# Scan products of an SSD mixer on four 64 by 64 tiles of TensorE, the second token block stored with its halves swapped, and the sample's products apart on 32 columns

## The chip, the cores and the metric

The kernel runs on one core of one Trainium2 chip. Its time is the device time of one execution in microseconds (us); a version's time is the median of several executions on the same chip. Beside it stands a profile: one execution, recorded instruction by instruction, of which the quoted lines are a part. Engines go by their names in it: PE is TensorE (PEld its weight loads), DVE VectorE, ACT ScalarE, POOL GpSimd, SP SyncE.

## The reference

One layer of a streaming encoder for 256 tokens of a new stream (the prompt) and the next 32 tokens of a running one (the sample), with shared weights. The input is normed and multiplied by w_in; the columns of the result go to a pooling mixer, to a gate z, and to an SSD mixer of 32 heads of 64 channels in two groups. Both mixers' outputs go through w_out and then a ConvFFN. What the change touches is the scan of the SSD mixer, which the reference works out in chunks of 64 tokens with a state carried from chunk to chunk:

```python
cb = jnp.einsum('bclgn,bcsgn->bcgls', Cc, Bc)
y_diag = jnp.einsum('bcgls,bcgjls,bcsgjp->bclgjp', cb, lmat, xc)
...
h_last, h_prev = lax.scan(step, h0, ...)
y_off = jnp.einsum('bclgn,bcgjpn,bcgjl->bclgjp', Cc, h_prev, jnp.exp(acum))
y = (y_diag + y_off).reshape(b, s, G, J, P) + D[..., None] * xh
```

Written out without chunks, a head's output at token l is the sum over all tokens s up to l of (C_l . B_s) exp(-decay between s and l) dt_s x_s, plus the old state's part and D x_l. For the prompt the old state is zero; the sample has one.

## The kernel before

**Layout.** Activations stand with channels on the 128 partitions and the 288 tokens (256 and 32) along the row. `project` (L171) multiplies a chunk of 256 weight columns with all tokens into two accumulators of the PSUM pool `acc_ps` (five buffers): each weight block arrives as f32 by DMA (`raw`), ScalarE rounds it to a high part `whi` (L151), VectorE subtracts for the low part `wlo` (L152), and TensorE runs three passes for each (L165). Of `whi` and `wlo` there are four buffers each. The splits get high priority, so the scheduler places them ahead of other work.

**The scan.** A group q is four heads, eight groups in all. For each: `ssd_tokens` (L617) loads x transposed to tokens on partitions into `xk` (three blocks: tokens 0 to 127, 128 to 255, and the last 128, of which the last 32 count; L619 and L620 on GpSimd's queue; three buffers). `ssd_first` (L598) broadcasts the decay sums over partitions (`gb`, L601), loads the old state `h0t` and forms `ce` (L610). `ssd_masks` (L623) multiplies x by dt (L636), forms the exponentials on ScalarE (L643, L646) and multiplies them by the masked products of B and C, `cbt` (L648). The mask `m` of a head has 416 columns: 256 for the first block of tokens against all later outputs, 128 for the second against its own, 32 for the sample.

**The products.** `run_pair` (L796) runs four times, each time for two groups: after the x chunk 7 and after the z chunks 1, 4 and 6. `ssd_products` runs for each group two pairs of heads, the two heads of a pair on the two halves of TensorE's columns: 256 columns (L668), 128 columns for the second block (L670), then the sample's 32 columns from new tokens (L672) and from the old state (L674). These are f32 products, and their place in TensorE's order is pinned to the written one. `ssd_add` (L684) then adds D x and the product into `xs` on VectorE, once for the prompt and once for the sample. After that come the gate (L758 takes z from its accumulator, L764 and L767 multiply) and the norm.

What the scheduler may move (VectorE, ScalarE, GpSimd) it orders itself; TensorE's order is that of the text. Of other work around the scan, L434, L435, L449, L454 and L455 are the causal convolution of x, and L211 its transpose on the way to the token layout.

Of the kernel before, what the change touches and what calls it, by code (L numbers as in the profile page):

```python
# [8 lines left out]
F32 = mybir.dt.float32  # L9
F32R = mybir.dt.float32r  # L10
AF = mybir.ActivationFunctionType
ALU = mybir.AluOpType
# [3 lines left out]
P = 128  # L16
TC = {"schedule_with_timeline_sim": True}
D_MODEL = 2048
NP_ = 256
NS = 32  # L20
NT = NP_ + NS
# [3 lines left out]
HEADS = 32  # L25
# [4 lines left out]
NF = D_FF // P  # L30
NXC = CONV // P
NU = D_POOL // P
BLK = ((0, P), (P, P), (NP_, NS))
WINDOWS = (2, 4, 8, 16)
HALF = NF // 2
# [33 lines left out]
def body(  # L69
# [23 lines left out]
    act, dve, pool, pe, sp = nc.scalar, nc.vector, nc.gpsimd, nc.tensor, nc.sync  # L93
# [9 lines left out]
    acc_ps = ctx.enter_context(tc.tile_pool(name="acc_ps", bufs=5, space=PSUM))  # L103
# [3 lines left out]
    def aux(shape, name):  # L107
        return aux_ps.tile(shape, F32, tag="aux", name=name)
# [21 lines left out]
    pin = tc.keep_in_program_order  # L130
# [90 lines left out]
    start = ExitStack()  # L221
# [41 lines left out]
    for name, n in COLS:  # L263
# [12 lines left out]
    tri = const.tile([P, P], F32, name="tri")  # L276
    pool.affine_select(
        out=tri, in_=ones, pattern=[[1, P]], compare_op=ALU.is_ge, fill=0.0, base=0, channel_multiplier=-1
# [79 lines left out]
    for i, (kb, n) in enumerate(CHUNKS):  # L358
# [26 lines left out]
        for q, (r, m, k, x) in enumerate(products):  # L385
            if i == len(CHUNKS) - 1 and q == 0:
                p_ = aux([P, NT], "prs")
# [9 lines left out]
                start=kb + k + r + x == 0, stop=kb + k == KD - 1 and r == 1,  # L397
            ))

    for k in range(KD):  # L400
        c = slice(HEADS * (k % 4), HEADS * (k % 4 + 1))
# [90 lines left out]
    with tc.high_priority(offset=EVAC):  # L492
        for i, v in enumerate(v4):
            c = slice(HEADS * i, HEADS * (i + 1))
# [34 lines left out]
    r = htile("r", tag="z")  # L529
# [26 lines left out]
    tok = mp.tile([P, 3, 2, HEADS], F32, name="tok")  # L556
    tokd = const.tile([P, 3, HEADS], F32, name="tokd")
    p_t = aux([P, 9 * HEADS], "ptok")
    p_tok = p_t.rearrange("p (b h) -> p b h", b=3)
# [4 lines left out]
    act.activation(elast, g[:, 415:416], AF.Exp)  # L564
    e_d = dram.tile([HEADS, 1], F32, name="e_d")
    sp.dma_start(out=e_d, in_=elast)
    dve.tensor_copy(tok, p_tok[:, :, : 2 * HEADS].rearrange("p b (r h) -> p b r h", r=2))
    dve.tensor_copy(tokd, p_tok[:, :, 2 * HEADS :])
    wq = side2.tile([P, HEADS], F32, name="wq")
    for j in range(3):  # L570
# [4 lines left out]
    for i in range(4):  # L575
        o = btile("bc")
# [3 lines left out]
    cbt = mp.tile([P, 2, MW], F32, name="cbt")  # L580
    pool.memset(cbt, 0.0)
    for gi in range(2):
        blocks_out(b_d, gi, bc[gi], mp, 2)
        p_ = aux([P, MW], "pcb")
        follow(pe.matmul(p_[:, 0:256], bc[gi][:, 0:P], bc[2 + gi][:, 0:NP_], start=True, stop=True))
        follow(pe.matmul(p_[:, 256:384], bc[gi][:, P:NP_], bc[2 + gi][:, P:NP_], start=True, stop=True))
        follow(pe.matmul(p_[:, 384:], bc[gi][:, TAIL:], bc[2 + gi][:, NP_:], start=True, stop=True))
        dve.tensor_tensor(cbt[:, gi, 0:128], p_[:, 0:128], tri, op=ALU.mult)
        dve.tensor_copy(cbt[:, gi, 128:256], p_[:, 128:256])
        dve.tensor_tensor(cbt[:, gi, 256:384], p_[:, 256:384], tri, op=ALU.mult)  # L590
        dve.tensor_tensor(cbt[P - NS :, gi, 384:], p_[P - NS :, 384:], tri[P - NS :, P - NS :], op=ALU.mult)


    xs = []
# [21 lines left out]

    def ssd_tokens(q):  # L617
        xk = mp.tile([P, 3, 2 * P], F32, tag="xk", bufs=3, name="xk")
        pool.dma_start(out=xk[:, 0:2, :], in_=xs_d[q][:NP_, :].rearrange("(b p) c -> p b c", p=P))  # L619
        pool.dma_start(out=xk[:, 2, :], in_=xs_d[q][TAIL:, :])  # L620
        tokens[q] = xk

# [29 lines left out]
            ssd_first(q + 1)  # L652
        return xw, m, h0t, ce

    def ssd_products(q, sample, xw, m, h0t, ce):

        rows_ = aux([P, 2 * NP_], "py")
        ys = []
        for i in range(2):
            y, y_s = rows_[:, NP_ * i : NP_ * (i + 1)], sample[:, NS * (2 * (q % 2) + i) :][:, :NS]  # L660
            ys.append((y, y_s))
            for k in range(4):
                for j in range(2):
                    h = 2 * i + j
                    c = slice(64 * j, 64 * j + 64)
                    f_ = slice(64 * h, 64 * h + 64)
                    if k == 0:
                        ins = pe.matmul(y[c, 0:256], xw[:, 0, f_], m[:, h, 0:256], start=True, stop=False)  # L668
                    elif k == 1:
                        ins = pe.matmul(y[c, 128:256], xw[:, 1, f_], m[:, h, 256:384], start=False, stop=True)  # L670
                    elif k == 2:
                        ins = pe.matmul(y_s[c, :], xw[:, 2, f_], m[:, h, 384:], start=True, stop=False)  # L672
                    else:
                        ins = pe.matmul(y_s[c, :], h0t[:, i, c], ce[:, h, :], start=False, stop=True)  # L674
                    pin(ins)
        return ys

    def ssd_add(q, ys):

        for i in range(2):  # L680
            t = 2 * q + i
            for c, y in zip((slice(0, NP_), slice(NP_, NT)), ys[i]):
                o = xs[t][:, c]
                dve.scalar_tensor_tensor(o, o, skip[:, t : t + 1], y, op0=ALU.mult, op1=ALU.add)  # L684

    def token_sums(p_, sq, first_, last_, pin=False):

# [100 lines left out]
    masks_ = {}  # L788
# [5 lines left out]

    def run_pair():
        sample = aux([P, 4 * NS], "py_s")  # L796
        ys = {q: ssd_products(q, sample, *masks_[q]) for q in sorted(masks_)}
        if quads:
            ssd_first(quads[0])
        for q in ys:  # L800
            ssd_add(q, ys[q])
            masks_.pop(q)
            done[0] = 2 * q + 1

# [650 lines left out]
```

## Time and profile before

| | |
|---|---|
| median of three executions | 1303.49 us (1303.31 to 1303.55) |
| span of the profiled execution, first to last instruction | 1302.0 us |
| TensorE busy | 1293.9 us (99%), mean granted clock 0.999 |
| VectorE / ScalarE / GpSimd busy | 897.9 (69%) / 672.8 (52%) / 255.8 us (20%) |
| a block of scan products (first row to the next projection row) | 148.19 to 151.85 us, the first of four |

The profiled execution's own time isn't recorded apart from its span; the median of the executions beside it is 1.5 us above the span. A row of the timeline has start, length, engine, line, operation and tiles; a row of the groups by form has the count, the shortest, median and longest duration in ns, and the first and last start. Rows of one line that overlap are drawn as one with a count (x4).

### The profile page before, as it was taken

The page shows a single profiled execution, that of the slowest core. Times are in us where ns is not written, and L with a number is a line of the kernel's source. Part 1 is how long each engine was busy: PE and PEld are TensorE (multiplying, and loading weights), DVE is VectorE, ACT ScalarE, POOL GpSimd, SP SyncE. Part 2 cuts the span into 40 slices and gives each one's busy share as a digit, 9 for nine tenths or more (in the row PEclk, how much of TensorE's full clock was granted, in tenths as well). Part 3 has the DMA queues.
Part 4 walks back from the last instruction along what each step waited for, and adds up shares of the span by engine and source line. Part 5 has one row for each costly group of instructions (what it writes and reads, how often), then busy time and mean ns, then how long its engine had stood idle before and what let it go on. Part 6 is the DMA issues. An engine that isn't in the chain of part 4 may idle for free.

```text
span 1302.0 us, 25255 instructions
## 1 busy us (share of the span) xinstructions
PE 1293.9 (99%) x10027; PEld 1285.0 (99%) x10027; DVE 897.9 (69%) x1526; ACT 672.8 (52%) x1013; POOL 255.8 (20%) x399
## 2 busy tenths in 40 slices
PE   9999999999999999999999999999999999999998
PEld 9999999999999999999999999999999999999997
DVE  8899988988655688867766744336666666755454
ACT  8455976656544567544444443334444444444442
POOL 3333312312232231212211100001121111201110
PEclk9999999999999999999999999999999999999999
DMA  9578976354776478767445445455545555466763
GB/s 360 168 220 242 303 244 215 130 183 162 253 208 223 139 202 268 196 182 210 165 162 167 165 165 175 160 173 184 172 163 166 173 174 169 162 231 190 215 182 114
DMA packets 110518, 251.78 MB, mean 193 GB/s; under 512 B 64960, under 2 KB 74080, under 8 KB 88128
## 3 DMA queue, kind: packets, MB, share of 16 engines
q1 hardware_dynamic: 104144, 233.52, 55.4%
q0 software_dynamic: 5824, 16.13, 4.3%
q8 instruction: 78, 1.28, 0.4%
q10 hardware_dynamic: 432, 0.52, 0.1%
q14 instruction: 40, 0.33, 0.1%
HBM read 237.13 MB, written 13.00 MB: 192 GB/s over the span
## 4 chain that ended last, share of the span: by engine, by line
PE 97%; issue 1%; DMA 1%; DVE 0%; ACT 0%; POOL 0%; POOLq 0%; ACTq 0%
PE acc L165 90%; PE acc L395 2%; PE acc_x L395 1%; PE acc_x L165 1%; PE py L668 1%; PE acc L1316 1%; DMA mg<-in_x_g 0%; PE acc L1317 0%; PE py L670 0%; DMA raw<-in_w_up 0%; DMA xg<-in_x_g 0%; PE acc_t L1339 0%; PE pst L1028 0%; PE acc L402 0%; PE py_s L674 0%
## 5 line engine op out<-in xcount | busy, mean ns | idle before, releaser
L152 DVE TENSOR_TENSOR wlo<-raw,whi 128x1024 fp32r<-128x1024 f32 (+1 forms) x396 | 473.3, 1197 | 297.8 <-ACT whi L151 295.5
L151 ACT ACTIVATE whi<-raw 128x1024 fp32r<-128x1024 f32 (+1 forms) x396 | 408.2, 1032 | 461.6 <-PE acc L165 372.0
L165 PE MATMUL acc<-hn,whi 128*128 128x288 f32 x2752 | 539.2, 294 | 0.8 <-ACT hn L1092 0.4
L165 PEld LDWEIGHTS acc<-hn,whi 128*128 128x128 f32 x2752 | 436.3, 188 | 2.1 <-ACT hn L1092 1.1
L165 PE MATMUL acc<-hn,wlo 128*128 128x288 f32 x1376 | 399.6, 291 | 0.0
L165 PEld LDWEIGHTS acc<-hn,wlo 128*128 128x128 f32 x1376 | 259.0, 188 | 0.0
L165 PE MATMUL acc<-fa,whi 128*128 128x288 f32 x1320 | 257.5, 293 | 0.0
L165 PE MATMUL acc<-xn,whi 128*128 128x288 f32 x1216 | 238.6, 294 | 0.0
L165 PEld LDWEIGHTS acc<-fa,whi 128*128 128x128 f32 x1320 | 209.1, 188 | 0.0
L165 PEld LDWEIGHTS acc<-xn,whi 128*128 128x128 f32 x1216 | 193.0, 188 | 0.6 <-issue 0.5
L165 PE MATMUL acc<-fa,wlo 128*128 128x288 f32 x660 | 192.1, 291 | 0.0
L165 PE MATMUL acc<-xn,wlo 128*128 128x288 f32 x608 | 177.4, 292 | 0.0
L165 PEld LDWEIGHTS acc<-fa,wlo 128*128 128x128 f32 x660 | 124.3, 188 | 0.0
L1142 POOL COPY fc_stage<-ebuf 128x4 f32<-128x4 f32 x88 | 26.9, 305 | 468.2 <-DVE ebuf L1141 446.2
L165 PEld LDWEIGHTS acc<-xn,wlo 128*128 128x128 f32 x608 | 114.5, 188 | 0.0
L165 PE MATMUL acc<-mixs,whi 128*128 128x288 f32 x512 | 100.2, 293 | 0.0
L1137 POOL COPY ebuf<-cols 128x2 f32<-128x2 f32 x88 | 74.4, 846 | 119.6 <-DVE fc L1148 88.3
L1148 DVE SCALAR_TENSOR_TENSOR fc<-ebuf,cols,fc 128x290 f32<-128x290 f32 x176 | 90.1, 516 | 3.7 <-ACT fc L1146 1.0
L1146 ACT ACTIVATE fc<-ebuf,cols 128x290 f32<-128x290 f32 x88 | 54.4, 623 | 73.2 <-DVE ebuf L1141 73.2
L165 PEld LDWEIGHTS acc<-mixs,whi 128*128 128x128 f32 x512 | 81.2, 188 | 0.0
L165 PE MATMUL acc<-mixs,wlo 128*128 128x288 f32 x256 | 74.6, 291 | 0.0
L165 PE MATMUL acc<-mixp,whi 128*128 128x288 f32 x256 | 50.1, 293 | 0.0
(310 smaller groups left out, 1239.8 us busy)
## 6 DMA issues: line engine op xcount, KB each, us to landing
raw<-in_w_up SPq DMA_DIRECT2D x80, 1024.0 KB, 5.1
raw<-in_w_in SPq DMA_DIRECT2D x38, 1024.0 KB, 5.5
raw<-in_w_down SPq DMA_DIRECT2D x32, 1024.0 KB, 4.9
raw<-in_w_out SPq DMA_DIRECT2D x22, 1024.0 KB, 5.2
raw<-in_w_down SPq DMA_DIRECT2D x16, 768.0 KB, 4.4
raw<-in_w_up SPq DMA_DIRECT2D x14, 512.0 KB, 4.3
gb<-g_d POOLq DMA_DIRECT2D x8, 832.0 KB, 6.6
raw<-in_w_first SPq DMA_DIRECT2D x5, 768.0 KB, 12.8
```

Of the source, the lines that this page charges most:

```text
L151: act.activation(hi, raw[:, k : k + n, :], AF.Copy)
L152: dve.tensor_tensor(lo, raw[:, k : k + n, :], hi.bitcast(F32), op=ALU.subtract)
L165: ins = pe.matmul(out, w, a[:, x, :], start=start and n == 0, stop=stop and n == 2)
L395: pin(pe.matmul(first[m], w[r][:, k, m * P : (m + 1) * P], xn[kb + k][:, x, :], start=kb + k + r + x == 0, stop=kb + k == KD - 1 and r == 1,))
L668: ins = pe.matmul(y[c, 0:256], xw[:, 0, f_], m[:, h, 0:256], start=True, stop=False)
L1137: pool.tensor_copy(e[:, 258:260], hist_f[:, :, i])
L1142: pool.tensor_copy(fc_stage[:, :, :, i], e[:, 256:324].rearrange("p (s c) -> p s c", c=34)[:, :, 0:2])
L1146: act.activation(c, e[:, 0:290], AF.Identity, bias=col["f_b"][:, i : i + 1], scale=f_w[:, 0, i : i + 1])
L1148: dve.scalar_tensor_tensor(c, e[:, r_ : r_ + 290], f_w[:, r_, i : i + 1], c, op0=ALU.mult, op1=ALU.add)
L1316: pin(pe.matmul(both, hi[:, c], f2[k][:, :, C1], start=k == 0, stop=end, skip_group_check=True))
```

## The change

The scan's products for the prompt run on four tiles of 64 rows by 64 columns in place of two of 128 by 64. The upper rows of the first block pass all 256 columns, the lower rows only the 192 of tokens from 64 on, into a PSUM tile of their own (`py_l`, from the accumulators' pool). The second block of tokens stands with its halves swapped: its upper rows hold tokens 192 to 255 and pass 64 columns, its lower rows tokens 128 to 191 and pass 128. For this `tok` and `cbt` are copied with swapped halves, once, and the load of x has a third DMA. `ssd_add` adds `py_l` in an addition of its own, 128 by 192. The sample's products leave the products' loop: `ssd_sample` runs after the products of both groups, in four tiles of 128 rows by 32 columns.

```diff
 NF = D_FF // P
 NXC = CONV // P
 NU = D_POOL // P
+UPPER = (slice(0, 64), slice(64, P))
+LOWER = UPPER[::-1]
 BLK = ((0, P), (P, P), (NP_, NS))
 WINDOWS = (2, 4, 8, 16)
 HALF = NF // 2
...
     act.activation(elast, g[:, 415:416], AF.Exp)
     e_d = dram.tile([HEADS, 1], F32, name="e_d")
     sp.dma_start(out=e_d, in_=elast)
-    dve.tensor_copy(tok, p_tok[:, :, : 2 * HEADS].rearrange("p b (r h) -> p b r h", r=2))
+    t_tok = p_tok[:, :, : 2 * HEADS].rearrange("p b (r h) -> p b r h", r=2)
+    dve.tensor_copy(tok[:, 0::2], t_tok[:, 0::2])
+    for to, of in (UPPER, LOWER):
+        dve.tensor_copy(tok[to, 1], t_tok[of, 1])
     dve.tensor_copy(tokd, p_tok[:, :, 2 * HEADS :])
     wq = side2.tile([P, HEADS], F32, name="wq")
     for j in range(3):
...
         follow(pe.matmul(p_[:, 384:], bc[gi][:, TAIL:], bc[2 + gi][:, NP_:], start=True, stop=True))
         dve.tensor_tensor(cbt[:, gi, 0:128], p_[:, 0:128], tri, op=ALU.mult)
         dve.tensor_copy(cbt[:, gi, 128:256], p_[:, 128:256])
-        dve.tensor_tensor(cbt[:, gi, 256:384], p_[:, 256:384], tri, op=ALU.mult)
+        for to, of in (UPPER, LOWER):
+            dve.tensor_tensor(cbt[to, gi, 256:384], p_[of, 256:384], tri[of, :], op=ALU.mult)
         dve.tensor_tensor(cbt[P - NS :, gi, 384:], p_[P - NS :, 384:], tri[P - NS :, P - NS :], op=ALU.mult)
 
 
...
 
     def ssd_tokens(q):
         xk = mp.tile([P, 3, 2 * P], F32, tag="xk", bufs=3, name="xk")
-        pool.dma_start(out=xk[:, 0:2, :], in_=xs_d[q][:NP_, :].rearrange("(b p) c -> p b c", p=P))
+        quarters = xs_d[q][:NP_, :].rearrange("(b p) c -> p b c", p=64)
+        pool.dma_start(out=xk[:64, 0:2, :], in_=quarters[:, 0::3, :])
+        pool.dma_start(out=xk[64:, 0:2, :], in_=quarters[:, 1:3, :])
         pool.dma_start(out=xk[:, 2, :], in_=xs_d[q][TAIL:, :])
         tokens[q] = xk
 
...
             ssd_first(q + 1)
         return xw, m, h0t, ce
 
-    def ssd_products(q, sample, xw, m, h0t, ce):
+    def ssd_products(q, xw, m):
 
         rows_ = aux([P, 2 * NP_], "py")
+        low_ = acc_ps.tile([P, 2 * 192], F32, tag="acc", name="py_l")
         ys = []
         for i in range(2):
-            y, y_s = rows_[:, NP_ * i : NP_ * (i + 1)], sample[:, NS * (2 * (q % 2) + i) :][:, :NS]
-            ys.append((y, y_s))
-            for k in range(4):
+            y, y_l = rows_[:, NP_ * i : NP_ * (i + 1)], low_[:, 192 * i : 192 * (i + 1)]
+            ys.append([y, y_l])
+            for r, b, n, o, at, first_ in (
+                (UPPER[0], 0, 256, y, 0, True), (LOWER[0], 0, 192, y_l, 0, True),
+                (UPPER[0], 1, 64, y, 192, False), (LOWER[0], 1, 128, y_l, 64, False),
+            ):
                 for j in range(2):
                     h = 2 * i + j
-                    c = slice(64 * j, 64 * j + 64)
-                    f_ = slice(64 * h, 64 * h + 64)
-                    if k == 0:
-                        ins = pe.matmul(y[c, 0:256], xw[:, 0, f_], m[:, h, 0:256], start=True, stop=False)
-                    elif k == 1:
-                        ins = pe.matmul(y[c, 128:256], xw[:, 1, f_], m[:, h, 256:384], start=False, stop=True)
-                    elif k == 2:
+                    to = (256 if b == 0 else 384) - n
+                    pin(pe.matmul(
+                        o[64 * j : 64 * j + 64, at : at + n], xw[r, b, 64 * h : 64 * h + 64], m[r, h, to : to + n],
+                        start=first_, stop=not first_,
+                    ))
+        return ys
+
+    def ssd_sample(q, sample, xw, m, h0t, ce):
+
+        ys = []
+        for i in range(2):
+            y_s = sample[:, NS * (2 * (q % 2) + i) :][:, :NS]
+            ys.append(y_s)
+            for old_ in range(2):
+                for g_ in range(4):
+                    h, c = 2 * i + g_ // 2, slice(32 * g_, 32 * g_ + 32)
+                    if old_:
+                        ins = pe.matmul(y_s[c, :], h0t[:, i, c], ce[:, h, :], start=False, stop=True)
+                    else:
+                        f_ = slice(P * i + 32 * g_, P * i + 32 * g_ + 32)
                         ins = pe.matmul(y_s[c, :], xw[:, 2, f_], m[:, h, 384:], start=True, stop=False)
-                    else:
-                        ins = pe.matmul(y_s[c, :], h0t[:, i, c], ce[:, h, :], start=False, stop=True)
                     pin(ins)
         return ys
 
-    def ssd_add(q, ys):
+    def ssd_add(q, ys, ys_s):
 
         for i in range(2):
             t = 2 * q + i
-            for c, y in zip((slice(0, NP_), slice(NP_, NT)), ys[i]):
+            for c, y in ((slice(0, NP_), ys[i][0]), (slice(NP_, NT), ys_s[i])):
                 o = xs[t][:, c]
                 dve.scalar_tensor_tensor(o, o, skip[:, t : t + 1], y, op0=ALU.mult, op1=ALU.add)
+            o = xs[t][:, 64:NP_]
+            dve.tensor_tensor(o, o, ys[i][1], op=ALU.add)
 
     def token_sums(p_, sq, first_, last_, pin=False):
 
...
 
     def run_pair():
         sample = aux([P, 4 * NS], "py_s")
-        ys = {q: ssd_products(q, sample, *masks_[q]) for q in sorted(masks_)}
+        ys = {q: ssd_products(q, *masks_[q][:2]) for q in sorted(masks_)}
+        ys_s = {q: ssd_sample(q, sample, *masks_[q]) for q in sorted(masks_)}
         if quads:
             ssd_first(quads[0])
         for q in ys:
-            ssd_add(q, ys[q])
+            ssd_add(q, ys[q], ys_s[q])
             masks_.pop(q)
             done[0] = 2 * q + 1
 
```

TensorE, the last pair of heads of the first block and what follows; py is the prompt's product, py_s the sample's. Before:

```order
L674 MATMUL py_s<-ce,h0t 64x32 x2
L668 MATMUL py<-m,xk 64x256 x2
L670 MATMUL py<-m,xk 64x128 x2
L672 MATMUL py_s<-m,xk 64x32 x2
L674 MATMUL py_s<-ce,h0t 64x32 x2
L165 MATMUL acc<-xn,whi 128x288
L165 MATMUL acc<-xn,wlo 128x288
```

And now, from the last pair's products to the sample's (the four pairs of the sample follow each other; the first two are shown, the projection comes after the fourth):

```order
L678 MATMUL py<-m,xk 64x256 x2
L678 MATMUL py_l<-m,xk 64x192 x2
L678 MATMUL py<-m,xk 64x64 x2
L678 MATMUL py_l<-m,xk 64x128 x2
L697 MATMUL py_s<-m,xk 32x32 x4
L694 MATMUL py_s<-ce,h0t 32x32 x4
L697 MATMUL py_s<-m,xk 32x32 x4
L694 MATMUL py_s<-ce,h0t 32x32 x4
```

The pair has four forms on two PSUM tiles in place of two on one, and the sample's rows have moved from each pair to the end of the block, four to a group of rows where two stood.

VectorE, after the first block, from the first z to the fourth split of weights (L152, now L154) behind the block. m and xk are the mask and the tokens of the next groups, conv and xs the convolution. Before:

```order
L758 TENSOR_TENSOR z<-acc,rstd 128x288
L648 TENSOR_TENSOR m<-m,cbt 128x1664
L636 TENSOR_TENSOR xk<-xk,tok 128x768
L454 SCALAR_TENSOR_TENSOR xs<-tanh,conv 128x256
L455 SCALAR_TENSOR_TENSOR xs<-tanh,conv 128x32
L758 TENSOR_TENSOR z<-acc,rstd 128x288
L152 TENSOR_TENSOR wlo<-raw,whi 128x1024
L449 SCALAR_TENSOR_TENSOR conv<-ebuf_169,pah,conv 128x291
L152 TENSOR_TENSOR wlo<-raw,whi 128x1024
```

Now:

```order
L783 TENSOR_TENSOR z<-acc,rstd 128x288
L213 STREAM_TRANSPOSE blocks<-xs 128x288
L154 TENSOR_TENSOR wlo<-raw,whi 128x1024
L783 TENSOR_TENSOR z<-acc,rstd 128x288
L154 TENSOR_TENSOR wlo<-raw,whi 128x1024
L451 SCALAR_TENSOR_TENSOR conv<-ebuf_169,pah,conv 128x291
L451 SCALAR_TENSOR_TENSOR conv<-ebuf_170,pah,conv 128x291
L656 TENSOR_TENSOR m<-m,cbt 128x1664
L644 TENSOR_TENSOR xk<-xk,tok 128x768
L451 SCALAR_TENSOR_TENSOR conv<-ebuf_169,pah,conv 128x291
L451 SCALAR_TENSOR_TENSOR conv<-ebuf_170,pah,conv 128x291
L154 TENSOR_TENSOR wlo<-raw,whi 128x1024 x2
```

Between the block's first addition into xs and this split stand eight steps of the convolution (L451) where five stood (L449), two transposes (L213) where one stood (L211), and the four new additions of py_l (L709), which come before the rows shown.

VectorE, after the second block, from the first split behind the first mask product. Before:

```order
L152 TENSOR_TENSOR wlo<-raw,whi 128x1024
L764 SCALAR_TENSOR_TENSOR z<-tanh_z,z 128x288
L758 TENSOR_TENSOR z<-acc,rstd 128x288
L152 TENSOR_TENSOR wlo<-raw,whi 128x1024
L767 TENSOR_TENSOR xs<-xs,z 128x288
L758 TENSOR_TENSOR z<-acc,rstd 128x288
L648 TENSOR_TENSOR m<-m,cbt 128x1664
L636 TENSOR_TENSOR xk<-xk,tok 128x768
L152 TENSOR_TENSOR wlo<-raw,whi 128x1024
```

Now, from the split that stands ahead of the first mask product:

```order
L154 TENSOR_TENSOR wlo<-raw,whi 128x1024
L656 TENSOR_TENSOR m<-m,cbt 128x1664
L644 TENSOR_TENSOR xk<-xk,tok 128x768
L783 TENSOR_TENSOR z<-acc,rstd 128x288
L154 TENSOR_TENSOR wlo<-raw,whi 128x1024
L783 TENSOR_TENSOR z<-acc,rstd 128x288
L154 TENSOR_TENSOR wlo<-raw,whi 128x1024
L656 TENSOR_TENSOR m<-m,cbt 128x1664
L644 TENSOR_TENSOR xk<-xk,tok 128x768
```

The third split stood behind both mask products (L648, L636) and now stands ahead of the second one (L656, L644).

## The prediction

> **What bounds the kernel now.** I read the page first: busy shares, clock, chain. Then the list of what TensorE waits for.
>
> ```profile
> PE 1293.9 (99%) x10027; PEld 1285.0 (99%) x10027; DVE 897.9 (69%) x1526; ACT 672.8 (52%) x1013; POOL 255.8 (20%) x399
> PEclk9999999999999999999999999999999999999999
> PE 97%; issue 1%; DMA 1%; DVE 0%; ACT 0%; POOL 0%; POOLq 0%; ACTq 0%
> PE acc_x L298 <- DVE busy L224: 1.3, 1, 1.3
> PE acc L165 <- ACT hn L1092: 0.4, 1, 0.4
> PE acc L165 <- ACT whi L151: 0.3, 1, 0.3
> ```
>
> TensorE is busy 99% of the span at full clock, the chain that ended last is 97% TensorE, and the longest wait is 1.3 us. So the time is TensorE's program laid end to end: the change is worth what it adds to or takes from TensorE's four blocks of scan products, unless another engine gets late enough to make TensorE wait. Those blocks are small; next come the groups by form of the tiles py and py_s (count: shortest/median/longest ns, first and last start) and one block in TensorE's timeline (start, length, group).
>
> ```profile
> L668 PE MATMUL py<-m,xk x64: 379/394/431, 148.2 to 250.6; 128*64 128x256 f32 x64
> L670 PE MATMUL py<-m,xk x64: 272/273/273, 148.7 to 250.9; 128*64 128x128 f32 x64
> L672 PE MATMUL py_s<-m,xk x64: 192/208/223, 148.9 to 251.0; 128*64 128x32 f32 x64
> L674 PE MATMUL py_s<-ce,h0t x64: 222/223/223, 149.0 to 251.1; 128*64 128x32 f32 x64
> L684 DVE SCALAR_TENSOR_TENSOR xs<-xs,cols,py x16: 467/470/473, 152.6 to 252.9; 128x256 f32<-128x256 f32 x16
> L684 DVE SCALAR_TENSOR_TENSOR xs<-xs,cols,py_s x16: 236/237/239, 155.2 to 254.1; 128x32 f32<-128x32 f32 x16
> ```
>
> ```profile
> 147.97 0.29 PE L165 MATMUL acc<-xn,wlo 128*128 128x288 f32 x1
> 148.19 0.65 PE L668 MATMUL py<-m,xk 128*64 128x256 f32 x4
> 148.68 0.39 PE L670 MATMUL py<-m,xk 128*64 128x128 f32 x4
> 148.90 0.26 PE L672 MATMUL py_s<-m,xk 128*64 128x32 f32 x4
> 148.98 0.29 PE L674 MATMUL py_s<-ce,h0t 128*64 128x32 f32 x4
> 149.10 0.63 PE L668 MATMUL py<-m,xk 128*64 128x256 f32 x4
> 149.56 0.39 PE L670 MATMUL py<-m,xk 128*64 128x128 f32 x4
> ...
> 151.63 0.29 PE L674 MATMUL py_s<-ce,h0t 128*64 128x32 f32 x4
> 151.85 0.40 PE L165 MATMUL acc<-xn,whi 128*128 128x288 f32 x1
> 152.09 0.30 PE L165 MATMUL acc<-xn,wlo 128*128 128x288 f32 x1
> 152.22 0.42 PE L165 MATMUL acc<-xn,whi 128*128 128x288 f32 x2
> ```
>
> Each of the 64 products of a form is one pass; a product in f32 takes two, so a form's x4 in the timeline is one pair of heads, and 16 pairs make 64. The pair takes .46 us for its 256 columns (149.10 to 149.56), .22 for its 128 (148.68 to 148.90) and .20 for the 32 sample columns (148.90 to 149.10): .88. Durations of single rows are longer than these steps since the two column tiles run side by side and the records overlap; I use starts only.
>
> **The change, part by part.**
>
> *Products.* A tile passes 256 + 128 = 384 columns in .68 us, the last 128 of them at .22/128 = 1.72 ns each. After it, the tile with the fuller half passes 256 + 64 = 320 and the other 192 + 128 = 320, so if the row halves run side by side a pair loses 64 columns: −64 × 1.72 = −.11, and 16 pairs −1.8 us. In every row above starts follow the program's order. If a product that waits for its own tile also holds up the next one, the lower half's 128 columns start only with the upper half's 64, at .46, and end at .68, .11 behind the upper tile; the following pairs shift by the same .11 and the lag is paid once per block: 4 × .11 = +.4. I take the lag: **−1.4**, with −1.8 as the better end. No product on half the rows is in the trace; its cost without overlap is a rival below.
>
> *Sample.* A pair had 8 passes on two tiles, four rounds in .20 us; it gets 16 passes on four tiles, again four rounds. What four tiles do to a round, the nearest rows show (TensorE's timeline at the dt columns; the groups of the small sum):
>
> ```profile
> 43.82 2.15 PE L402 MATMUL acc<-xg,w_dt 128*32 128x288 f32 x32
> 45.90 0.40 PE L165 MATMUL acc<-xn,whi 128*128 128x288 f32 x1
> ...
> 1290.48 0.24 PE L1243 MATMUL psum_f<-ones,fsq 128*32 128x1 f32 x8
> ...
> L1243 PE MATMUL psum_f<-ones,fsq x8: 170/180/192, 1290.5 to 1290.6; 128*32 128x1 f32 x8
> ```
>
> L402's 32 passes of 288 columns stand on four tiles: 8 rounds in at most 45.90 − 43.82 = 2.08, .26 each or .90 ns a column; two tiles at L668 take .46/2/256 = .90. So a round of four takes as long as a round of two, and the sample costs **0**. The ends: if half as many weight columns to load shortened a round (.05) by a third, −.07 a pair and −1.1 in all; if entries cannot follow each other faster than now (8 in .20), twice the time, a rival below.
>
> *Mode switches.* A block is entered and left once, before as after; new is one change inside it, from 64 by 64 to 128 by 32. Entry: .22 us from the last L165 to the first L668 where 152.09 to 152.22 is the usual .13, and .49 for the first 256 columns against .46: .12. Exit: 151.63 to 151.85 is .22 where L674 is otherwise followed after .12, and the next L165 after .24 instead of .13: .21. I take the middle, .17, four times: **+.7** (.5 to .9).
>
> *Sum:* −1.4 + 0 + .7 = **−.7 us** on TensorE.
>
> *VectorE* gets 16 additions of 128 by 192. Between L684's two sizes lie 234 ns for 224 columns, so 237 + 160 × 1.04 = 404 ns at most: 6.5 us in all, 1.6 in each block, and it has 31% of the span free over the whole. But the kernel's splits of weights (L152) are made just ahead of TensorE's use. The stages after blocks 1 and 2, in VectorE's timeline and TensorE's:
>
> ```profile
> 159.15 0.52 DVE L449 SCALAR_TENSOR_TENSOR conv<-ebuf,pah,conv 128x291 f32<-128x291 f32 x1
> 163.02 0.47 DVE L211 STREAM_TRANSPOSE blocks<-xs 128x288 f32<-128x288 f32 x1
> 168.79 1.21 DVE L152 TENSOR_TENSOR wlo<-raw,whi 128x1024 fp32r<-128x1024 f32 x1
> ...
> 174.12 0.29 PE L165 MATMUL acc<-xn,wlo 128*128 128x288 f32 x1
> ...
> 195.09 1.88 DVE L648 TENSOR_TENSOR m<-m,cbt 128x1664 f32<-128x1664 f32 x1
> 198.38 1.21 DVE L152 TENSOR_TENSOR wlo<-raw,whi 128x1024 fp32r<-128x1024 f32 x1
> 199.51 0.45 DVE L764 SCALAR_TENSOR_TENSOR z<-tanh_z,z 128x288 f32<-128x288 f32 x1
> 199.87 0.29 PE L165 MATMUL acc<-xn,wlo 128*128 128x288 f32 x1
> ```
>
> The fourth split after block 1 ends at 170.00 and is used at 174.12: 4.1 us in hand. By the new order the additions (1.6), three convolution steps (L449, 3 × .5) and a transpose (L211, .5) stand ahead of it: 3.6, so some .5 us is left, less .2 if TensorE comes that much earlier. After block 2 the split that ends at 199.59 has only .28 in hand; in the new order the two multiplications of the second masks stand behind it and not ahead, which gives it more than the 1.9 of L648. So I cost VectorE at 0; the cover is thin after block 1, and is a rival.
>
> *GpSimd* gets one more load of tokens for each of eight groups, at up to .72 us:
>
> ```profile
> 179.22 0.72 POOL L619 DMA_DIRECT2D xk<-xs_d  x1 [2.21 <-PE py_s L674]
> 179.93 0.56 POOL L620 DMA_DIRECT2D xk<-xs_d  x1
> 183.18 0.53 POOL L601 DMA_DIRECT2D gb<-g_d  x1 [0.93 <-ACT m L643]
> ```
>
> That is 5.8 us more on an engine that is busy 20% of the span. Behind it in the queue stands the broadcast at L601, which waited .93 for ScalarE after the loads were issued and so covers one more. The first of the loads waited 2.21 for a sample product to free the buffer; the samples of both groups now come at the block's end, for the first group two pairs or 1.8 us later. The copies with halves swapped are done once, ahead of the blocks. py_l takes two of the five accumulators of the projection's chunks until the additions, whose last four start at 155.2, 3.4 us after the block; a chunk is 48 passes of .13 or 6 us, and three accumulators are left for it. All of these I cost at 0, at most .5 together.
>
> **The rivals.**
>
> *Short rounds (faster).* Rounds of four narrow loads take less than rounds of two: −1.1 beside the −.7: 1301.7. For it: L1243 starts its 8 passes within .24 − .17 = .07. Against it: L402 is no quicker a column.
>
> *Sample bound by the feed.* Before, passes start every .20/8 = 25 ns. If that is the rate at which TensorE is fed, and not two tiles' rounds, a block's 64 passes take 64 × .025 = 1.6 us where 32 take .8: +.8 × 4 = +3.2, so −.7 + 3.2 = +2.5: 1306.0. For it: the equal spacing. Against: L1243's eight within .07, though these are too few to show a rate that lasts. The Trainium skill, "TensorE: Matmul & The Clock Gate", section "Wait — 56ns, not 53.3ns?", says that start to start never drops below about 25 ns however few the columns; the sample's .20 for 8 agrees, L1243's rows do not.
>
> *A split comes late.* After block 1 some .3 us is left. If one step more than I counted gets ahead of the split in time, a mask product of 1.88 being the largest, TensorE waits 1.88 − .3 = 1.6: 1304.4. For it: the thin cover. Against: TensorE's waits for splits of weights in the whole run are .3.
>
> *Row halves do not overlap (slower).* Then the four steps of a pair follow each other: 256 + 192 + 64 + 128 = 640 columns at .68/384 = 1.77 ns are 1.13 for .68, +.45 × 16 = +7.2, with the switches +7.9: 1311.4. It decides once less than about 280 of the 320 columns that the lower half adds run beside the upper half's. For it: no row here has two products on different rows at once. Against: the two column tiles run side by side, x4 in the time of two. The skill's "TensorEngine Tiling (Array Packing)", section "Key Properties", says that tiles load and multiply independently; no row of this profile shows it for row halves.
>
> *The change does not do what it says:* the products' order on TensorE shows it does, so this has no chance of its own.
>
> **How the numbers follow.** The profiled span is 1302.0 and the median of three runs 1303.49; 1.5 us lie around the span and the change touches none of that. Span 1302.0 − .7 = 1301.3, time **1302.8**. Chances: forecast .44 (1302.2 to 1303.3), short rounds .13, feed .17, late split .13, no overlap .13. The range leaves out the last and a little beside it: 1301.0, the forecast with the better ends (−1.8 + .5 − 1.1 = −2.4), to 1306.2, the feed with .2 for the smaller costs. About 0.2%, 2.6 us, is what a measurement of this kernel can tell from no change: faster by more needs short rounds and cheap switches together, .12; slower by more is no overlap and a part of the feed's case, .19; the same .69.
>
> **What would show it.** In TensorE's timeline after the change: a pair of heads every .57 us in the products (1.13 if the halves do not overlap), the lower form starting beside the upper; a gap of about .17 ahead of the 128 by 32 passes; eight sample rows in .8 us a block (1.6 if the feed binds, .5 if rounds are short); blocks of 3.5 instead of 3.66 (148.19 to 151.85). In the list of TensorE's waits: L165 for a split still under .5 us. In VectorE's groups: 16 additions of about .4. Wrong would be: a block longer than 5 us, or waits for splits that grow with no change in the blocks.

## The result, and the profile after

| | before | changed |
|---|---|---|
| median of 21 executions | 1303.61 us | 1301.67 us |
| span of the profiled execution | 1302.0 us | 1300.8 us |
| a block of scan products (blocks 2 to 4) | 3.66 us | 3.06 us |
| from block 1 to 2, 2 to 3, 3 to 4 | 25.22, 37.70, 25.55 us | 25.23, 37.71, 25.56 us |

The ratio is 0.9985, with a 95% interval of 0.9978 to 0.9991: 1.9 us faster, between 1.2 and 2.9. (One execution of the changed kernel, at 2669.73 us, stands apart from the other 20, which lie between 1300.79 and 1302.99.) A block is measured here and below from the start of its first product to the start of the next row of the projection.

The page of the changed kernel, its shares of busy time and the chain that ended last:

```profile
PE 1292.3 (99%) x10283; PEld 1284.9 (99%) x10283; DVE 900.2 (69%) x1546; ACT 670.9 (52%) x1013; POOL 255.0 (20%) x407
PE 95%; issue 2%; DMA 1%; ACT 1%; POOL 0%; DVE 0%; SPq 0%; POOLq 0%; ACTq 0%
```

TensorE still bounds it, with 1.6 us less busy time (1292.3 against 1293.9) and 256 more passes. What the groups by form show of the tiles py, py_l and py_s (count: shortest/median/longest ns):

```profile
L678 PE MATMUL py<-m,xk x128: 216/297/427, 149.1 to 249.3; 64*64 64x256 f32 x64, 64*64 64x64 f32 x64
L678 PE MATMUL py_l<-m,xk x128: 269/296/373, 149.1 to 249.2; 64*64 64x192 f32 x64, 64*64 64x128 f32 x64
L697 PE MATMUL py_s<-m,xk x128: 196/196/217, 151.4 to 250.0; 128*32 128x32 f32 x128
L697 PEld LDWEIGHTS py_s<-m,xk x128: 106/109/113, 151.4 to 249.9; 128*32 128x32 f32 x128
L709 DVE TENSOR_TENSOR xs<-xs,py_l x16: 335/340/344, 156.9 to 255.7; 128x192 f32<-128x192 f32 x16
```

And TensorE's timeline in block 2 of the changed kernel:

```profile
177.73 0.43 PE L678 MATMUL py<-m,xk 64*64 64x256 f32 x2
177.74 0.54 PE L678 MATMUL py_l<-m,xk 64*64 64x192 f32 x4
177.99 0.38 PE L678 MATMUL py<-m,xk 64*64 64x256 f32 x2
178.12 0.28 PE L678 MATMUL py_l<-m,xk 64*64 64x128 f32 x2
178.21 0.22 PE L678 MATMUL py<-m,xk 64*64 64x64 f32 x2
...
178.54 0.38 PE L678 MATMUL py<-m,xk 64*64 64x256 f32 x2
...
179.09 0.38 PE L678 MATMUL py<-m,xk 64*64 64x256 f32 x2
...
179.91 0.23 PE L678 MATMUL py<-m,xk 64*64 64x64 f32 x2
180.06 0.27 PE L697 MATMUL py_s<-m,xk 128*32 128x32 f32 x8
180.15 0.25 PE L694 MATMUL py_s<-ce,h0t 128*32 128x32 f32 x8
180.21 0.25 PE L697 MATMUL py_s<-m,xk 128*32 128x32 f32 x8
180.28 0.25 PE L694 MATMUL py_s<-ce,h0t 128*32 128x32 f32 x8
...
180.78 0.40 PE L167 MATMUL acc<-xn,whi 128*128 128x288 f32 x1
```

Three readings. The second pass of the 256 columns starts every .55 us (177.99, 178.54, 179.09), so a pair of heads takes .55 where its prompt part took .68: both row halves run at once. The lower rows' 128 columns start at 178.12, ahead of the upper rows' 64 at 178.21, though the text has them behind: here a product on a free tile started before one that stands ahead of it in the order. And the sample's groups of eight passes on four tiles follow each other every .065 us; before, on two tiles, four passes took .09 to .12. The whole sample, 180.06 to 180.78 with its exit, is .72 us.

In the list of TensorE's waits of the changed kernel nothing stands between 148 and 300 us, as before. VectorE is close to it, as the windows view (busy of PE, PEld, DVE, ACT, POOL, then the granted clock) and its timeline show behind block 1:

```profile
152.50:177.70 25.20, 25.20 (x193) 25.07 (x192) 25.20 (x46) 19.67 (x40) 7.69 (x13) 1.00 0.90 266
...
172.14 2.35 DVE L154 TENSOR_TENSOR wlo<-raw,whi 128x1024 fp32r<-128x1024 f32 x2
...
174.78 0.29 PE L167 MATMUL acc<-xn,wlo 128*128 128x288 f32 x1
```

VectorE had no idle time at all in those 25.2 us. The fourth split behind block 1 (counted from the additions on) is the first of the two from 172.14 and takes 1.21 as single ones do, to 173.35. Its use stood at 174.12 before and moves with block 2's start (177.07, now 177.73), by .66, to 174.78: 1.4 us was left of the 4.1.

In the profiled execution block 1 took 3.40 us instead of 3.06; that is taken up below. Its start, too, came later (149.10 against 148.19). TensorE's program ahead of it is the same; VectorE's copies with swapped halves stand there, but with the same copies the start lay anywhere between 147.92 and 148.93 in the experiments on the changed kernel, and at 148.40 and 148.53 in the two without them. So this .9 is not put down to the change.

### The profile page after: what moved, and what is told of

Read it like the earlier page. It is cut to its first block, busy times and chain, and to the rows that moved or that the text cites. A ratio compares the mean times of both kernels' runs of the same rounds, so it can differ in the third digit from the quotient of the medians.

```text
span 1300.8 us, 25801 instructions
## 1 busy us (share of the span) xinstructions
PE 1292.3 (99%) x10283; PEld 1284.9 (99%) x10283; DVE 900.2 (69%) x1546; ACT 670.9 (52%) x1013; POOL 255.0 (20%) x407
## 4 chain that ended last, share of the span: by engine, by line
PE 95%; issue 2%; DMA 1%; ACT 1%; POOL 0%; DVE 0%; SPq 0%; POOLq 0%; ACTq 0%
PE acc L167 89%; PE acc L397 1%; DMA raw<-in_w_first 1%; PE acc_x L167 1%; PE acc_x L397 1%; PE acc L1342 1%; PE acc L1343 0%; DMA mg<-in_x_g 0%; PE py L678 0%; PE py_l L678 0%; PE acc_t L1365 0%; ACT w L330 0%; POOL ho L1073 0%; PE acc L404 0%; DVE xr L1385 0%
## 5 line engine op out<-in xcount | busy, mean ns | idle before, releaser
L154 DVE TENSOR_TENSOR wlo<-raw,whi 128x1024 fp32r<-128x1024 f32 (+1 forms) x396 | 472.7, 1196 | 285.6 <-ACT whi L153 284.7
L153 ACT ACTIVATE whi<-raw 128x1024 fp32r<-128x1024 f32 (+1 forms) x396 | 407.7, 1032 | 445.4 <-PE acc L167 362.6
L1163 POOL COPY ebuf<-cols 128x2 f32<-128x2 f32 x88 | 71.7, 815 | 114.8 <-DVE fc L1174 98.8
```

Source lines behind the costliest of these rows:

```text
L153: act.activation(hi, raw[:, k : k + n, :], AF.Copy)
L154: dve.tensor_tensor(lo, raw[:, k : k + n, :], hi.bitcast(F32), op=ALU.subtract)
L1163: pool.tensor_copy(e[:, 258:260], hist_f[:, :, i])
```

## The experiments

Each experiment has one profiled execution and its time, beside one execution of the kernel before on the same chip. One time doesn't tell half a microsecond apart, but blocks 2 to 4 agree within .002 us in each kernel, so blocks are what is compared. Here is block 2 of each, from its first product to the next projection row; the last column is taken from the trace to the nanosecond:

| kernel | from | to | block |
|---|---|---|---|
| before | 177.07 | 180.72 | 3.655 |
| changed | 177.73 | 180.78 | 3.057 |
| e1, changed, sample on 64 columns | 176.57 | 179.97 | 3.393 |
| e2, before, sample on 32 columns at the end | 177.23 | 180.70 | 3.469 |
| e3, before, sample at the end | 177.27 | 180.93 | 3.655 |
| e4, changed, all columns | 177.64 | 181.12 | 3.479 |
| e7, changed, lower 128 ahead | 177.22 | 180.28 | 3.057 |
| e8, changed, sample behind each pair | 177.93 | 181.79 | 3.863 |
| e9, changed, sample on 64 by 64 | 178.34 | 181.58 | 3.239 |
| e10, changed, two narrow tiles | 176.12 | 179.08 | 2.966 |

**e1, the sample on 64 columns.** In `ssd_sample`:

```diff
-                for g_ in range(4):
-                    h, c = 2 * i + g_ // 2, slice(32 * g_, 32 * g_ + 32)
+                for j in range(2):
+                    h, c = 2 * i + j, slice(64 * j, 64 * j + 64)
...
-                        f_ = slice(P * i + 32 * g_, P * i + 32 * g_ + 32)
+                        f_ = slice(64 * h, 64 * h + 64)
```

> The changed kernel with the sample's products still at the block's end, but on two tiles of 64 columns as before (8 passes a pair, 32 a block). Measure is a block from its first product to the next projection row: 3.66 us before, 3.06 in the changed kernel's blocks 2 to 4. If four narrow tiles are what shortened the sample, each pair takes .20 again instead of about .13 and the block is 3.3 (3.25 to 3.4). If the gathering at the block's end did it, the block stays at 3.0 to 3.1.

1301.32 us (before 1303.26), block 3.393: .336 more than the changed kernel. The narrow tiles shorten the sample, the gathering doesn't. TensorE's timeline in its block 1, each row four passes on two tiles, two rounds (a round is one pass on each tile):

```profile
150.43 0.29 PE L694 MATMUL py_s<-ce,h0t 128*64 128x32 f32 x4
150.55 0.29 PE L697 MATMUL py_s<-m,xk 128*64 128x32 f32 x4
150.66 0.29 PE L694 MATMUL py_s<-ce,h0t 128*64 128x32 f32 x4
```

A row follows the other every .117 on average, so a round takes .058.

**e2 and e3, the kernel before with the sample at the block's end,** on 32 and on 64 columns; the prompt's products as before.

```diff
-            for k in range(4):
+            for k in range(2):
...
-        ys = {q: ssd_products(q, sample, *masks_[q]) for q in sorted(masks_)}
+        ys = {q: ssd_products(q, *masks_[q][:2]) for q in sorted(masks_)}
+        ys_s = {q: ssd_sample(q, sample, *masks_[q]) for q in sorted(masks_)}
```

> The kernel before with its prompt products (128 by 64, 384 columns) and only the sample changed: at the block's end, on four tiles of 32 columns. If the columns left out are worth .54 a block and the sample .2, the block is 2.7 for the products, .1 for the switch and .7 for the sample with the exit: 3.5. If the sample's move is worth nothing alone: 3.66.

> The kernel before with its products and the sample's 64 columns, only gathered at the block's end. By the rounds' theory nothing changes: 3.66 (3.6 to 3.7). If interleaving itself cost time at each turn from 32 to 256 columns (.46 for the 256 columns against .44 at 1.72 ns a column), a block is 3.55 to 3.6.

e3 (1303.06 us) gives 3.655, to the third digit the block of before: the move alone is worth nothing. e2 (1303.19 us) gives 3.469. With e1 that makes four blocks out of two choices, and three unknowns: columns left out C, narrow sample N, and a change of tiles inside the block S, which is there in all but e3 and is taken as equal in the three others. C + S = 3.393 − 3.655 = −.262; N + S = 3.469 − 3.655 = −.186; C + N + S = 3.057 − 3.655 = −.598. So **S = +.150, C = −.412, N = −.336** a block, or +.6, −1.65 and −1.34 us in all four.

**e4, all columns on the four tiles.** `py_l` grows to 256 columns, of which the addition takes the last 192.

```diff
-                (UPPER[0], 0, 256, y, 0, True), (LOWER[0], 0, 192, y_l, 0, True),
-                (UPPER[0], 1, 64, y, 192, False), (LOWER[0], 1, 128, y_l, 64, False),
+                (UPPER[0], 0, 256, y, 0, True), (LOWER[0], 0, 256, y_l, 0, True),
+                (UPPER[0], 1, 128, y, 128, False), (LOWER[0], 1, 128, y_l, 128, False),
```

> The changed kernel with nothing left out of the diagonal blocks: each of the four tiles passes 256 and 128 columns (384 in place of 320; the added ones meet zeros of the mask). If the gain is the columns, a pair takes 384 x 1.70 = .65 in place of .545 and a block 3.06 + 4 x .11 = 3.5. If four tiles themselves are quicker than two, the block stays near 3.1. If the fixed part were large: between.

1304.42 us, block 3.479: .422 more. That is C measured another way. Four tiles with 384 columns each take what two with 384 take (e2: 3.469), within .01 a block, so C is the columns and little else. But the time is 1.2 us above the kernel before (1303.26), though its blocks are .18 shorter: from block 2 to 3 it took 39.14 in place of 37.71. Its list of TensorE's waits and the timelines of TensorE and VectorE:

```profile
PE acc L167 <- DVE wlo L154: 0.6, 1, 0.6
...
192.09 1.89 DVE L656 TENSOR_TENSOR m<-m,cbt 128x1664 f32<-128x1664 f32 x1 [0.19 <-ACT m L654]
193.90 0.95 DVE L644 TENSOR_TENSOR xk<-xk,tok 128x768 f32<-128x768 f32 x1
...
196.66 1.22 DVE L154 TENSOR_TENSOR wlo<-raw,whi 128x1024 fp32r<-128x1024 f32 x1 [1.44 <-ACT whi L153]
...
196.89 0.42 PE L167 MATMUL acc<-xn,whi 128*128 128x288 f32 x2
197.94 0.40 PE L167 MATMUL acc<-xn,wlo 128*128 128x288 f32 x1 [0.62 <-DVE wlo L154]
```

A split came late by .6: the prediction's rival, in another kernel and one stage on. ScalarE's rounding L153 held it; VectorE was idle for 1.44 ahead of the split. ScalarE itself was late: the last of the twelve exponentials ahead of it (L651) ended at 195.67, in the changed kernel at 193.77, 1.6 earlier counted from the block's end. It had stood idle twice for VectorE's gate products (L792: 1.75 and 1.07), so the delay may go back to VectorE's order; no run takes this apart.

**e5 and e6, no addition of py_l, and each made four times.**

```diff
             o = xs[t][:, 64:NP_]
-            dve.tensor_tensor(o, o, ys[i][1], op=ALU.add)
+            for _ in range(4):
+                dve.tensor_tensor(o, o, ys[i][1], op=ALU.add)
```

> The changed kernel without the 16 new additions of py_l on VectorE (the lower rows' part of the prompt's product is left out of the output). If the additions are hidden, blocks and the waits of TensorE for splits stay as in the changed kernel (waits for splits .2 in all) and the span outside of the blocks is the same within .2. If they cost TensorE something unseen, the stages between the blocks are shorter by .3 or more.

> The changed kernel with each of the 16 additions made four times (48 more of .34: 16 us of VectorE, 4.1 a block; py_l is counted four times over). If the cover after block 1 is the .3 to .5 us that the prediction worked out, TensorE now waits for splits behind block 1 by about 3 us or more, and the span grows by 3 to 8. If the scheduler has more room than was counted, the waits stay under 1 us.

e5 (1301.56 us; before 1302.98): the stages between the blocks stay at 25.22, 37.71 and 25.56. The 16 additions are hidden there, to the hundredth. e6 took 1309.82 us, 8 more. Its list of TensorE's waits from 148 to 300 us:

```profile
PE acc L167 <- DVE z L784: 4.5, 3, 2.7
PE acc L167 <- DVE wlo L154: 0.6, 1, 0.6
```

The size was at the upper end of what was expected, the place not. It is not the split that TensorE mostly waits for but z, which VectorE takes out of the accumulators that the next chunk needs. And behind block 1 only 1.9 us is lost (27.16 in place of 25.23) and behind block 2 another 2.2 (39.87 in place of 37.71); about half, some 4.4 by the spans, is lost behind block 4, with one wait. TensorE's timeline there:

```profile
267.23 0.29 PE L167 MATMUL acc<-xn,wlo 128*128 128x288 f32 x1
270.23 0.53 PE L167 MATMUL acc<-xn,whi 128*128 128x288 f32 x2 [2.71 <-DVE z L784]
```

**e7, the lower rows' 128 columns ahead of the upper rows' 64,** the two tuples swapped in the table of e4's diff.

> The changed kernel with the lower rows' 128 columns ahead of the upper rows' 64 in the order. If a product that waits for its tile holds up the next one (the prediction's lag of .11 a block), the order 256, 192, 128, 64 starts each as its tile comes free and a block gets .1 shorter. If tiles take their products from the queue on their own, as the changed kernel's rows suggest (the lower 128 columns start at 149.49, ahead of the upper 64 at 149.58, against the written order), nothing changes: 3.06.

1301.85 us, block 3.057: no change. The written order doesn't matter here.

**e8, the sample behind each pair:** the lines of `ssd_sample` are moved into the loop over pairs of `ssd_products`.

> The changed kernel with the sample on 32 columns directly behind each pair's products, so that a block changes from 64 by 64 to 128 by 32 and back four times in place of once: six switches more. At .09 each (the changed kernel's gap ahead of the sample) a block grows by .5 to 3.6; at the .17 that the prediction took, by 1.0 to 4.1. If a switch costs nothing of its own, the block stays at 3.1.

1304.68 us (before 1302.98), block 3.863: .806 more for six changes of tiles, .134 each. This is near S = .150.

**e9, the sample on the prompt's tiles.** In `ssd_sample`, for each head, in place of two products on 128 rows:

```diff
+                    if k == 0:
+                        f_ = slice(64 * h, 64 * h + 64)
+                        ins = pe.matmul(o_[c, :], xw[l, 2, f_], m[l, h, 384:], start=True, stop=False)
+                    elif k == 1:
+                        ins = pe.matmul(y_s[c, :], h0t[u, i, c], ce[u, h, :], start=True, stop=True)
+                    else:
+                        ins = pe.matmul(o_[c, :], h0t[l, i, c], ce[l, h, :], start=False, stop=True)
```

> The changed kernel with the sample on the prompt's own tiles of 64 by 64, so that a block has no change of tiles inside: the upper rows take half of the old state, the lower rows the other half and the new tokens, into a strip behind py_l that the same addition takes in (128 by 224). It saves the switch (.15 a block by the runs so far). But a pair then has four rounds with 64 weight columns on the lower tiles; at the .053 of a round that the runs with 64 columns showed (.85 for 16 rounds) against .037 on four narrow tiles (.593) the sample costs .26 more: block 3.06 - .15 + .26 = 3.2. If rounds on 64 rows are as short as narrow ones: 2.9, which would beat the changed kernel by .6 us.

Block 3.239, as the first case had it: rounds on 64 weight columns are long on 64 rows too. But the time is 1307.10 us (before 1302.71), and the stages between blocks are 27.18 and 41.53 long in place of 25.23 and 37.71. Its list of TensorE's waits from 148 to 300 us, and the place behind block 1:

```profile
PE acc L167 <- DVE wlo L154: 2.0, 2, 1.3
PE acc L167 <- ACT whi L153: 1.0, 1, 1.0
...
167.41 1.89 DVE L656 TENSOR_TENSOR m<-m,cbt 128x1664 f32<-128x1664 f32 x1
169.21 0.95 DVE L644 TENSOR_TENSOR xk<-xk,tok 128x768 f32<-128x768 f32 x1
170.08 0.52 DVE L451 SCALAR_TENSOR_TENSOR conv<-ebuf,pah,conv 128x291 f32<-128x291 f32 x1
170.51 0.45 DVE L786 TENSOR_TENSOR z<-acc,rstd 128x288 f32<-128x288 f32 x1
170.88 2.35 DVE L154 TENSOR_TENSOR wlo<-raw,whi 128x1024 fp32r<-128x1024 f32 x2
...
172.16 0.40 PE L167 MATMUL acc<-xn,wlo 128*128 128x288 f32 x1 [1.32 <-DVE wlo L154]
```

The split that TensorE waits for is the third behind the additions (after 163.04 and 164.62). In the changed kernel three splits were made ahead of the second multiplications of mask and tokens, here two. VectorE has nearly the same to do (903.6 us busy against 900.2); the scheduler placed it otherwise. Behind block 2, waits of .97 and .73 follow each other within 2 us, and what came after them is taken up at the end.

**e10, two of the four narrow tiles.** Half of the sample's channels are left out, and py_s is zeroed ahead.

```diff
-                for g_ in range(4):
+                for g_ in (0, 2):
```

> The changed kernel with only two of the four narrow tiles used in a round (the other half of the sample's channels is left out, those outputs are zeroed ahead): 32 passes a block as before, 16 rounds, but each with 32 weight columns. If the narrow loads shorten a round, the sample takes .59 or less from first to last start, as on four tiles. If instead a round on two tiles always takes .053 and it is the four tiles that help, it takes .85. If the feed of products bounds it (16.7 ns a product by the later rows of the changed kernel's sample, 16 products a block), it falls to about .3 to .4.

1299.97 us, block 2.966. The sample takes .50 us from first to last start, against .59 on four tiles and .90 on two tiles of 64 columns (e1). So a round is shorter with 32 weight columns than with 64, and the number of tiles hardly matters. Its rows in TensorE's timeline, each four passes on two tiles, two rounds:

```profile
178.73 0.23 PE L697 MATMUL py_s<-m,xk 128*32 128x32 f32 x4
178.79 0.24 PE L694 MATMUL py_s<-ce,h0t 128*32 128x32 f32 x4
178.85 0.23 PE L697 MATMUL py_s<-m,xk 128*32 128x32 f32 x4
178.92 0.23 PE L694 MATMUL py_s<-ce,h0t 128*32 128x32 f32 x4
```

.063 for two rounds is .031 a round; e1 has .058. That it is the weight load that shrinks fits its records (L697, median 113 ns here, 138 in e1), but no run varies the load alone. The four tiles take .09 more than the two for twice the passes; if that is the rate at which TensorE is fed, it binds at most a little.

**e11, the changed kernel once more.**

> The changed kernel as it is, profiled a second time. In its first profile one product of block 1's sample started .34 us late with no engine to wait for (the list of waits puts it to issue), and the 147.6 us ahead of block 1 were .9 longer than before. If both belong to the execution and not to the change, block 1 is now near 3.06 and the start differs by some tenths either way; if they belong to the change, they are there again with .34 and .9. Blocks 2 to 4 should read 3.06 to the hundredth.

1302.02 us, blocks 2 to 4 at 3.057, the first start at 148.65. But block 1 took 3.62, and its rows show where:

```profile
PE py_s L694 <- issue: 0.4, 1, 0.4
...
151.49 0.26 PE L694 MATMUL py_s<-ce,h0t 128*32 128x32 f32 x6
152.12 0.22 PE L694 MATMUL py_s<-ce,h0t 128*32 128x32 f32 x1 [0.36 <-issue]
```

One product at the end of block 1's sample starts late, with no engine to wait for. Block 1 was longer than the others by .34 and .56 in the changed kernel's two profiles, by .23 in e5, by .04 in e7 and .03 in e8, and by nothing in e4, e6 and e10. So it showed only in kernels whose block has 128 passes, not in all of them, and its size belongs to the execution. One reading is that instructions arrive late there. In each profile one packet of 16 KB on the instruction queue starts near block 1 and takes .92 to .94 us. Counted from the block's start it began at −.40 in e6 and .42 in e4, with nothing lost; at .75 and .76 in e7 and e8, with .04 and .03 lost; at .81 in the changed kernel's first profile (.34), .92 in e5 (.23) and 1.28 in e11 (.56). In the kernels with fewer passes it began as late as 1.19 (e9) with nothing lost. That fits the reading, but no run moved the packet, and the cause stays open.

## Why the prediction was right, and where its sum was not

The sign, the place and the range held: 1301.67 lies between 1301.0 and 1306.2, the gain is in the four blocks, and the three stages between them are as long as before within about .01 us. But the forecast's size was off, 1302.8 from −.7 us where the runs gave −1.9, and the interval of 1.2 to 2.9 leaves .7 out: the rival with **short rounds**, at 1301.7 with a chance of .13, is the one that came. The range held because its lower end had been set with that rival's −1.1 in it, not because the forecast was near.

- *The sample, 0* was the term that failed. It measured −1.34 us (N). The step was to read from L402, 32 passes of 288 columns on four tiles, that a round of four takes as long as a round of two. That is so with many columns to pass (e2 and e4, within .01 a block). But L402's round of 288 columns takes .26 us, and a weight load, .11 us by its own record, can lie under it. With 32 columns to pass the round went with the weight columns: .058 with 64 (e1), .031 with 32 (e10). The row used as a witness had another limit than the row it was to stand for. L1243, with one column to pass, was the better witness, and was set aside as too short. The better end of −1.1, a guess at a shorter load, was near the measured value.
- *Products, −1.4* measured −1.65 (C, e4 −1.69). The columns were right; the lag of .11 a block was not. The prediction had starts in the program's order from rows with all tiles equally loaded. The changed kernel's rows show the lower tile going ahead (178.12 against 178.21), and e7 that the written order is nothing. Without the lag the sum had −1.8.
- *Switches, +.7* measured +.6 (S; e8 .134 each). Right.
- *VectorE, 0* held, with more cover than was worked out: 1.4 us behind block 1 where the prediction had .3. Counted from the end of block 1, the use of the fourth split stands where it stood (22.3 us), and the split ends 2.7 us later, not 3.6: an addition took .34, not .40, and VectorE had been idle for .63 ahead of one split before, which the sum left out. e5 shows that the additions cost nothing between the blocks, e6 that four times as many cost 8 us.
- *GpSimd and the copies, 0* held: the stages between the blocks didn't move.

So −1.65 − 1.34 + .6 = −2.4 is the sum by measured terms, and −2.05 in the profiled execution, where block 1 lost .34 of it; the median's −1.9 lies near, with an interval that takes both in.

Of the rivals, **no overlap** fell with the first rows: 640 columns would take 1.13 us a pair, not .55. **The feed** fell in its price: eight passes start within .065, 8 ns each, not 25. By the Trainium skill, "TensorE: Matmul & The Clock Gate", section "Wait — 56ns, not 53.3ns?", starts are never closer than about 25 ns; these rows, with four tiles in turn, have three times that rate (and 16 ns a product, if its two passes count as one). **The late split** didn't come in the changed kernel, but did in e4 and e9, where VectorE has nearly the same work in another order. The prediction priced a wait at its length; in e4 a wait of .62 made the stage 1.43 longer.

## What to carry to other kernels

Before a duration is carried from one row to another shape, ask what limits each of them. Here a round with many columns to pass took as long on four tiles as on two, while a round with 32 to pass went with the weight columns, and halving these paid although twice as many products were issued. Leaving columns out paid by the column on tiles that ran side by side, and a change of tiling cost .13 to .15 us each time, so gather what shares a tiling. Where a second engine has only a microsecond to spare, an edit that hardly adds to its work can still reorder it, as in e4 and e9: look at the waits of each variant before its time is read as the edit's price.

## What the runs showed of the hardware

- A late operand can cost TensorE more than the wait. In e4, behind the .62 wait, passes of the projection follow each other a little slower for the rest of the stage, at a granted clock of 1.00. TensorE's timeline, ahead of the wait and behind it, three passes from row to row of wlo:

```profile
196.37 0.29 PE L167 MATMUL acc<-xn,wlo 128*128 128x288 f32 x1
196.76 0.29 PE L167 MATMUL acc<-xn,wlo 128*128 128x288 f32 x1
...
198.83 0.30 PE L167 MATMUL acc<-xn,wlo 128*128 128x288 f32 x1
199.23 0.30 PE L167 MATMUL acc<-xn,wlo 128*128 128x288 f32 x1
```

  .39 became .40, and over some 165 passes up to block 3 that is about half a microsecond. It isn't so each time: in e9, behind the 1.32 wait, passes kept .13 apart. Why, no run shows.

- A longer wait costs the clock. In e6, TensorE started no pass from 267.23 to 270.23, and the windows view behind it has

```profile
270.70:274.20 3.50, 3.50 (x17) 3.50 (x16) 3.50 (x10) 1.75 (x4) 0.00 (x0) 0.52 0.14 23
275.00:285.00 10.00, 10.00 (x77) 10.00 (x76) 6.08 (x12) 4.99 (x7) 5.46 (x6) 1.00 0.62 198
```

  a granted clock of .52 for 3.5 us, 17 passes where 27 would fit, then 1.00 again. That adds 1.3 us to the 3.0. Two shorter waits in a row did the same: in e9, behind the waits of .97 and .73 that ended at 195.36 and 196.62, the view has a granted clock of .59 from 197 to 200 us and .85 from 200 to 203, and the stage took 41.53 in place of 37.71, about twice what the waits alone come to. Single waits of 1.2 (e6, behind block 2) and 1.32 (e9, behind block 1) left it at 1.00.
